# Encoder trunk on one core: a third chunk pair with seven block products in w_down, and two weight sums formed by adding DMAs

## Chip, cores and metric

The kernel runs on one core of one Trainium2 chip. The metric is the device time of one execution in microseconds (us), here the median of several runs.

## What is computed

Two residual layers, each a gated mix of three token mixers followed by an MLP with squared ReLU, and a final RMSNorm. `x` is 256 tokens by 2048 channels, float32. The change touches the last matrix product of the MLP, `w_down`:

```python
for l in range(DEPTH):                       # 2 layers
    ...
    x = x + merged @ w_out[l]
    h2 = rms_norm(x, norm2_g[l])
    u = jax.nn.relu(h2 @ w_up[l])            # 256 x 8192
    x = x + (u * u) @ w_down[l]              # w_down: 8192 x 2048
return rms_norm(x, final_g)
```

## The kernel before, in words

**Weights.** Every weight matrix is streamed once from HBM in tiles of 256 rows x 512 columns (512 KB), two chunks of 128 rows side by side in one `raw` tile (`fetch`, L165, on SP's DMA queue, four `raw` buffers). Float32 products are made from two halves of reduced width: `lead` (L171, L172) lets ScalarE round a tile to `whi` and VectorE subtract to get the rest, `wlo`. A block product is then three matmuls of 128x128 by 128x512 (`product`, L210 to L212): high by high, high by low, low by high.

**Order of the work.** `slots` is a list of tiles in the order of their use, written out by `add_unit` and `add_pair`. `run_steps` walks it: for each slot it issues the slot's matmuls and, in the middle, calls `ahead`, which converts the tile three slots further on (`AHEAD`, four `whi`/`wlo` buffers) and then fetches into every `raw` buffer that a conversion has released. Every engine executes its instructions in the order in which they are issued. Work besides the matrix products (splitting `U`, transposes, the sums named below) lies in generators, of which `side_work` runs one piece in each plain slot.

**w_up and w_down.** The 8192 features are taken in four quarters `q`. A quarter has four units of `w_up` (32 slots, `by_feature`, L228 and L229), which leave `U`, and then `w_down` for these 2048 features: two pairs of column blocks (`add_pair`), each 8 steps `s` of 256 rows. In the last quarter of a layer only one pair is done so, and the other two column blocks are plain units. That is 7 pairs in a layer, 14 in all.

**Seven products.** One step of a pair is a 2x2 by 2x2 product of blocks: two token halves, two chunks of 128 rows, two column blocks of 512. A plain step makes 8 block products in two slots (24 matmuls). For `s` in `SEVEN` it makes 7, in four slots a, b, c, d (2, 2, 2 and 1 products, 21 matmuls; `seven`). This needs four sums of token blocks (`block_sums`, L355, kept in `SU`) and four sums of weight blocks: `convert` makes them on VectorE in `T`, two at slot a (L191, L192) and two at slot b (L196, L197), from the two `raw` tiles `b0` and `b1`, which stay in use until slot b and slot d. Four of the seven products are shared sums of the results; they are kept in PSUM banks `P` over the steps and put together once per pair, by `middle_down` (L765, L770, L774), a generator that starts after the last seven-product step. `after_pair` (L797) then adds the four accumulators to `x`.

```python
SEVEN = (1, 3)
...
def ahead(i):
    convert(min(i + AHEAD, 2 * i + 1))
    fetch(st["free"] - 1 + RAW_BUFS)
```

Of the kernel before, what the change touches and what calls it, by code (L numbers as in the profile page):

```python
# [39 lines left out]
SEVEN = (1, 3)  # L40
# [31 lines left out]
def encoder_trunk(ctx: ExitStack, tc: tile.TileContext, I, out: bass.AP):  # L72
# [62 lines left out]
    slots, raws = [], []  # L135
    st = {"dma": 0, "cv": 0, "free": 0}
    raw_t, hl_t = {}, {}

    def add_raw(w, r, c):
        raws.append(w[r:r + 256, c:c + BLK])  # L140
        return len(raws) - 1
# [6 lines left out]
    def add_pair(w, r0, c0, nkc, act, sums, half, middle, after):  # L148

        u = {"act": act, "after": after, "n": nkc, "form": "pair", "sums": sums, "half": half, "middle": middle}  # L150
        for s in range(nkc // 2):
            r = [add_raw(w, r0 + 256 * s, c0 + n * BLK) for n in range(2)]
            if s in SEVEN:
                q = {"r": r}
# [6 lines left out]
    def fetch(upto):  # L161
        while st["dma"] <= min(upto, len(raws) - 1):
            j = st["dma"]
            t = raw_p.tile([128, 2, BLK], F32, tag="raw", name="raw")
            nc.sync.dma_start(out=t, in_=raws[j].rearrange("(k p) f -> p k f", p=128))  # L165
            raw_t[j] = t
            st["dma"] += 1

# [5 lines left out]
    def convert(upto):  # L174
        while st["cv"] <= min(upto, len(slots) - 1):
# [7 lines left out]
            else:  # L183
                q = sl["q"]
                if kind == "a":
                    q["b0"], q["b1"] = [raw_t.pop(r) for r in q["r"]]
                    q["T"] = one.tile([128, 4, BLK], F32, tag="merged", name="tsum")
                b0, b1, T = q["b0"], q["b1"], q["T"]
                if kind == "a":
                    nc.scalar.activation(out=hi, in_=b0, func=ACTF.Copy)  # L190
                    nc.vector.tensor_tensor(out=T[:, 1, :], in0=b1[:, 0, :], in1=b0[:, 0, :], op=ALU.subtract)  # L191
                    nc.vector.tensor_tensor(out=T[:, 0, :], in0=b1[:, 1, :], in1=T[:, 1, :], op=ALU.subtract)  # L192
                    nc.vector.tensor_tensor(out=lo, in0=b0, in1=hi.bitcast(F32), op=ALU.subtract)
                elif kind == "b":
                    nc.scalar.activation(out=hi, in_=T[:, 0:2, :], func=ACTF.Copy)
                    nc.vector.tensor_tensor(out=T[:, 2, :], in0=b1[:, 1, :], in1=b1[:, 0, :], op=ALU.subtract)  # L196
                    nc.vector.tensor_tensor(out=T[:, 3, :], in0=b0[:, 1, :], in1=T[:, 0, :], op=ALU.subtract)  # L197
                    nc.vector.tensor_tensor(out=lo, in0=T[:, 0:2, :], in1=hi.bitcast(F32), op=ALU.subtract)
                elif kind == "c":
                    lead(hi, lo, T[:, 2:4, :])  # L200
                else:
# [79 lines left out]
    def ahead(i):  # L281
        convert(min(i + AHEAD, 2 * i + 1))
        fetch(st["free"] - 1 + RAW_BUFS)

# [9 lines left out]
    def seven(u, s, kind, a, w, i):  # L294

# [53 lines left out]
    def block_sums(dst, e):  # L349
# [3 lines left out]
        for j, x0, x1, op in ((0, a21, a22, ALU.add), (1, f[:, 0, :], a11, ALU.subtract),  # L353
                              (2, a11, a21, ALU.subtract), (3, a12, f[:, 1, :], ALU.subtract)):
# [376 lines left out]
    def after_up(n):  # L731
        def f(ps):
            c = L["c"]
            if n == 0:
                c["U"] = one.tile([128, KD, 2, S], FR, tag="Y", name="U")
            U = c["U"]
# [20 lines left out]
    def middle_down(n):  # L757

        def pieces(P):
# [8 lines left out]
            def plus(tag, a, b):  # L768
# [271 lines left out]
```

## Time and profile before

| | |
|---|---|
| three runs | 2869.48 us median (2869.01 to 2870.3) |
| the profiled execution | 2870.48 us, span 2868.7 us, so 1.8 us lie around the span |
| TensorE (PE) busy | 2849.0 us, 99% of the span, granted clock 0.999 |
| VectorE (DVE), ScalarE (ACT), GpSimd (POOL) busy | 62%, 49%, 4% |
| bytes moved | 540.00 MB, 188 GB/s over the span |

Matmuls overlap: one of 512 columns is shown as 0.39 us long, and the next starts about 0.23 us after it. What a matmul costs is therefore read from the distance of starts, not from its length. The same holds in a small way for DVE and ACT, whose instructions overlap by up to a tenth of a microsecond.

### The profile page before, as it was taken

The page shows a single profiled execution, that of the slowest core. Times are in us where ns is not written, and L with a number is a line of the kernel's source. Part 1 is how long each engine was busy: PE and PEld are TensorE (multiplying, and loading weights), DVE is VectorE, ACT ScalarE, POOL GpSimd, SP SyncE. Part 2 cuts the span into 40 slices and gives each one's busy share as a digit, 9 for nine tenths or more (in the row PEclk, how much of TensorE's full clock was granted, in tenths as well). Part 3 has the DMA queues.
Part 4 walks back from the last instruction along what each step waited for, and adds up shares of the span by engine and source line. Part 5 has one row for each costly group of instructions (what it writes and reads, how often), then busy time and mean ns, then how long its engine had stood idle before and what let it go on. Part 6 is the DMA issues. An engine that isn't in the chain of part 4 may idle for free.

```text
span 2868.7 us, 35998 instructions
## 1 busy us (share of the span) xinstructions
PE 2849.0 (99%) x13858; PEld 2374.5 (83%) x13858; DVE 1778.8 (62%) x2201; ACT 1403.5 (49%) x1782; POOL 104.6 (4%) x104
## 2 busy tenths in 40 slices
PE   8999999999999999999999999999999999999998
PEld 7888888888888888888888888888888888888887
DVE  5455554555677686776644654555556876868675
ACT  5455445444554454544544554454444544444453
POOL 1000001010000000000000000011100000000001
PEclk9999999999999999999999999999999999999999
DMA  7656666665566566565676666656555565655654
GB/s 235 196 152 191 195 179 173 185 189 181 180 199 197 177 207 191 190 191 185 195 211 183 156 196 195 183 160 190 188 186 184 183 196 186 213 179 195 200 184 175
DMA packets 275804, 540.00 MB, mean 188 GB/s; under 512 B 16852, under 2 KB 17038, under 8 KB 275504
## 3 DMA queue, kind: packets, MB, share of 16 engines
q1 hardware_dynamic: 271344, 523.63, 57.7%
q0 software_dynamic: 3952, 13.28, 3.1%
q8 instruction: 108, 1.77, 0.3%
q10 hardware_dynamic: 336, 0.80, 0.1%
q14 instruction: 64, 0.52, 0.1%
HBM read 535.51 MB, written 2.13 MB: 187 GB/s over the span
## 4 chain that ended last, share of the span: by engine, by line
PE 98%; DVE 1%; ACT 0%; DMA 0%; issue 0%; POOLq 0%; DVEq 0%; POOL 0%; SPq 0%
PE acc L210 22%; PE acc L212 22%; PE acc L211 22%; PE acc L228 17%; PE acc L229 8%; PE psum L211 1%; PE psum L212 1%; PE psum L210 1%; PE ob L536 1%; PE scb L504 0%; PE xt L383 0%; PE sca L562 0%; PE oa L596 0%; PE qkt L453 0%; PE etb L526 0%
## 5 line engine op out<-in xcount | busy, mean ns | idle before, releaser
L172 DVE TENSOR_TENSOR wlo<-raw,whi 128x1024 fp32r<-128x1024 f32 (+1 forms) x964 | 1173.6, 1222 | 840.8 <-ACT whi L171 833.6
L171 ACT ACTIVATE whi<-raw 128x1024 fp32r<-128x1024 f32 (+1 forms) x964 | 1002.4, 1045 | 907.2 <-PE acc L212 556.3
L228 PE MATMUL acc<-H,whi 128*128 128x512 f32 x2048 | 724.7, 399 | 0.0
L229 PE MATMUL acc<-H,wlo 128*128 128x256 f32 x2048 | 575.2, 281 | 0.0
L210 PE MATMUL acc<-whi,H 128*128 128x512 f32 x1408 | 564.8, 401 | 0.0
L212 PE MATMUL acc<-whi,H 128*128 128x512 f32 x1408 | 550.1, 391 | 0.0
L211 PE MATMUL acc<-wlo,H 128*128 128x512 f32 x1408 | 549.5, 390 | 0.3
L228 PEld LDWEIGHTS acc<-H,whi 128*128 128x128 f32 x2048 | 384.9, 188 | 96.1 <-DVE x L705 0.6
L229 PEld LDWEIGHTS acc<-H,wlo 128*128 128x128 f32 x2048 | 387.1, 189 | 0.3
L210 PE MATMUL acc<-whi,U 128*128 128x512 f32 x856 | 334.0, 390 | 2.2 <-ACT junk L393 2.2
L211 PE MATMUL acc<-wlo,U 128*128 128x512 f32 x856 | 333.2, 389 | 0.0
L212 PE MATMUL acc<-whi,U 128*128 128x512 f32 x856 | 333.2, 389 | 0.0
L210 PEld LDWEIGHTS acc<-whi,H 128*128 128x128 f32 x1408 | 265.0, 188 | 58.6 <-issue 8.1
L212 PEld LDWEIGHTS acc<-whi,H 128*128 128x128 f32 x1408 | 264.6, 188 | 56.8
L211 PEld LDWEIGHTS acc<-wlo,H 128*128 128x128 f32 x1408 | 265.2, 188 | 52.6 <-DVE wlo L172 1.4
L210 PEld LDWEIGHTS acc<-whi,U 128*128 128x128 f32 x856 | 160.7, 188 | 36.3 <-ACT junk L393 3.0
L212 PEld LDWEIGHTS acc<-whi,U 128*128 128x128 f32 x856 | 160.7, 188 | 33.5
L211 PEld LDWEIGHTS acc<-wlo,U 128*128 128x128 f32 x856 | 160.7, 188 | 32.9
L210 PE MATMUL acc<-whi,M 128*128 128x512 f32 x256 | 101.3, 396 | 0.0
L212 PE MATMUL acc<-whi,M 128*128 128x512 f32 x256 | 99.9, 390 | 0.0
L211 PE MATMUL acc<-wlo,M 128*128 128x512 f32 x256 | 99.6, 389 | 0.0
L678 POOL TENSOR_TENSOR merged<-merged,gp 128x512 f32<-128x512 f32 x32 | 54.3, 1717 | 397.4 <-DVE gp L677 397.4
(190 smaller groups left out, 2278.1 us busy)
## 6 DMA issues: line engine op xcount, KB each, us to landing
raw<-in_w_in_dram SPq DMA_DIRECT2D x352, 512.0 KB, 4.4
raw<-in_w_up_dram SPq DMA_DIRECT2D x256, 512.0 KB, 4.2
raw<-in_w_down_dram SPq DMA_DIRECT2D x256, 512.0 KB, 4.5
raw<-in_w_out_dram SPq DMA_DIRECT2D x64, 512.0 KB, 3.8
raw<-in_w_proj_a_dram SPq DMA_DIRECT2D x24, 512.0 KB, 4.6
raw<-in_w_proj_b_dram SPq DMA_DIRECT2D x24, 512.0 KB, 4.2
raw<-in_w_proj_c_dram SPq DMA_DIRECT2D x16, 512.0 KB, 4.5
biasb<-bias_d POOLq DMA_DIRECT2D x16, 384.0 KB, 9.2
```

Of the source, the lines that this page charges most:

```text
L171: nc.scalar.activation(out=hi, in_=src, func=ACTF.Copy)
L172: nc.vector.tensor_tensor(out=lo, in0=src, in1=hi.bitcast(F32), op=ALU.subtract)
L210: nc.tensor.matmul(o, a[0], hi[:, kk, :], start=first, stop=False)
L211: nc.tensor.matmul(o, a[0], lo[:, kk, :], start=False, stop=False)
L212: nc.tensor.matmul(o, a[1], hi[:, kk, :], start=False, stop=last)
L228: nc.tensor.matmul(ps[j], hi[:, kk, fs], a[:, kc, :, :], start=first, stop=False)
L229: nc.tensor.matmul(ps[j][:, S:2 * S], lo[:, kk, fs], a[:, kc, 0, :], start=False, stop=last)
L536: nc.tensor.matmul(o[:, g, :], eT[:, 2 * g + kc, :], c["vb"][:, kc, col:col + 64], start=kc == 0, stop=kc == 1)
L678: nc.gpsimd.tensor_tensor(out=mg[:, t, cols], in0=mg[:, t, cols], in1=e, op=ALU.add)
```

## The change

`SEVEN` becomes (1, 3, 4): three of the eight steps of each pair are made with seven products. The signs of the block sums are changed so that the weight sums need only additions, and two of the four weight sums are no longer made on VectorE. `fetch_sums` loads both blocks of the first chunk into the middle of `T` (SP's queue), and a second DMA, issued by GpSimd, reads the two chunks of the second column block from HBM and adds them to what lies there. The second DMA writes where the first wrote, so it waits for it. `T` has two buffers and is loaded two seven-product steps ahead; the load into a buffer waits for slot c of the step that used it. VectorE makes the other two sums at slot a, and nothing at slot b. Of `b1` only the second chunk is still needed and loaded (256 KB in place of 512). `middle_down` is cut into six pieces in place of five.

```diff
-SEVEN = (1, 3)
+SEVEN = (1, 3, 4)
...
-            r = [add_raw(w, r0 + 256 * s, c0 + n * BLK) for n in range(2)]
+            r = [add_raw(w, r0 + 256 * s, c0 + n * BLK, half=s in SEVEN and n == 1) for n in range(2)]
             if s in SEVEN:
-                q = {"r": r}
+                q = {"r": r, "w": w[r0 + 256 * s:r0 + 256 * (s + 1), c0:c0 + 2 * BLK], "i": len(summed)}
+                summed.append(q)
...
-            nc.sync.dma_start(out=t, in_=raws[j].rearrange("(k p) f -> p k f", p=128))
+            src, half = raws[j]
+            if half:
+                nc.sync.dma_start(out=t[:, 1, :], in_=src[128:256, :])
+            else:
+                nc.sync.dma_start(out=t, in_=src.rearrange("(k p) f -> p k f", p=128))
...
+    def fetch_sums():
+
+        while L.get("T") is not None and st["sum"] < min(st["used"] + 2, len(summed)):
+            q = summed[st["sum"]]
+            if q["i"] >= L["T_end"]:
+                return
+            T = q["T"] = L["T"][:, q["i"] % 2]
+            w = q["w"]
+            nc.sync.dma_start(out=T[:, 1:3, :], in_=w[0:128, :].rearrange("p (n f) -> p n f", n=2))
+            nc.gpsimd.dma_start(out=T[:, 1:3, :], in_=w[:, BLK:2 * BLK].rearrange("(k p) f -> p k f", p=128),
+                                accum_op=ALU.add)
+            st["sum"] += 1
...
                 if kind == "a":
                     nc.scalar.activation(out=hi, in_=b0, func=ACTF.Copy)
-                    nc.vector.tensor_tensor(out=T[:, 1, :], in0=b1[:, 0, :], in1=b0[:, 0, :], op=ALU.subtract)
-                    nc.vector.tensor_tensor(out=T[:, 0, :], in0=b1[:, 1, :], in1=T[:, 1, :], op=ALU.subtract)
+                    nc.vector.tensor_tensor(out=T[:, 0, :], in0=T[:, 2, :], in1=b0[:, 0, :], op=ALU.add)
+                    nc.vector.tensor_tensor(out=T[:, 3, :], in0=T[:, 0, :], in1=b0[:, 1, :], op=ALU.add)
                     nc.vector.tensor_tensor(out=lo, in0=b0, in1=hi.bitcast(F32), op=ALU.subtract)
                 elif kind == "b":
-                    nc.scalar.activation(out=hi, in_=T[:, 0:2, :], func=ACTF.Copy)
-                    nc.vector.tensor_tensor(out=T[:, 2, :], in0=b1[:, 1, :], in1=b1[:, 0, :], op=ALU.subtract)
-                    nc.vector.tensor_tensor(out=T[:, 3, :], in0=b0[:, 1, :], in1=T[:, 0, :], op=ALU.subtract)
-                    nc.vector.tensor_tensor(out=lo, in0=T[:, 0:2, :], in1=hi.bitcast(F32), op=ALU.subtract)
+                    lead(hi, lo, T[:, 0:2, :])
                 elif kind == "c":
                     lead(hi, lo, T[:, 2:4, :])
+                    st["used"] += 1
...
         convert(min(i + AHEAD, 2 * i + 1))
         fetch(st["free"] - 1 + RAW_BUFS)
+        fetch_sums()
...
+                if "T" not in c:
+                    c["T"] = True
+                    L["T"] = one.tile([128, 2, 4, BLK], F32, tag="merged", name="tsum")
+                    L["T_end"] = len(summed) * (c["l"] + 1) // DEPTH
```

How the issue order moves is shown at two places. The first is SP's DMA queue around the first pair of a layer (`raw` with 128x2x512 is a whole tile, with 128x512 the half of `b1`; `tsum` is the load into `T`). Before, SP issues nothing but whole tiles:

```order
L165 DMA raw<-in_w_out_dram 128x2x512 x32
L165 DMA raw<-in_w_up_dram 128x2x512 x32
L165 DMA raw<-in_w_down_dram 128x2x512 x32
L165 DMA raw<-in_w_up_dram 128x2x512 x32
L165 DMA raw<-in_w_down_dram 128x2x512 x32
```

Now, from the `w_up` units on to the tiles of steps 6 and 7 of the first pair and on into the second:

```order
L182 DMA tsum<-in_w_down_dram 128x1024 x2
L170 DMA raw<-in_w_up_dram 128x2x512 x16
L170 DMA raw<-in_w_down_dram 128x2x512 x3
L168 DMA raw<-in_w_down_dram 128x512
L170 DMA raw<-in_w_down_dram 128x2x512 x2
L182 DMA tsum<-in_w_down_dram 128x1024
L170 DMA raw<-in_w_down_dram 128x2x512
L168 DMA raw<-in_w_down_dram 128x512
L170 DMA raw<-in_w_down_dram 128x2x512
L168 DMA raw<-in_w_down_dram 128x512
L182 DMA tsum<-in_w_down_dram 128x1024
L170 DMA raw<-in_w_down_dram 128x2x512 x2
```

After this last row comes another `tsum` and then seven whole tiles, the first of them those of step 6. So the first two loads into `T` lie in the middle of `w_up`, and in a pair one stands ahead of the tiles of step 3 (issued after slot c of step 1), one ahead of those of step 5 (after slot c of step 3) and one ahead of those of step 6 (after slot c of step 4).

The second place is VectorE in the same pair. Before, slots b of step 1 to b of step 3, with one `U` split of the side work between:

```order
L196 TENSOR_TENSOR tsum<-raw 128x512
L197 TENSOR_TENSOR tsum<-raw,tsum 128x512
L198 TENSOR_TENSOR wlo<-tsum,whi 128x1024
L343 TENSOR_TENSOR U<-u,U 128x2x256
L172 TENSOR_TENSOR wlo<-tsum,whi 128x1024
L172 TENSOR_TENSOR wlo<-raw,whi 128x512
L172 TENSOR_TENSOR wlo<-raw,whi 128x1024 x2
L191 TENSOR_TENSOR tsum<-raw 128x512
L192 TENSOR_TENSOR tsum<-raw,tsum 128x512
L193 TENSOR_TENSOR wlo<-raw,whi 128x1024
```

Now, slots a of step 3 to d of step 4:

```order
L208 TENSOR_TENSOR tsum<-tsum,raw 128x512
L209 TENSOR_TENSOR tsum<-tsum,raw 128x512
L210 TENSOR_TENSOR wlo<-raw,whi 128x1024
L190 TENSOR_TENSOR wlo<-tsum,whi 128x1024 x2
L190 TENSOR_TENSOR wlo<-raw,whi 128x512
L208 TENSOR_TENSOR tsum<-tsum,raw 128x512
L209 TENSOR_TENSOR tsum<-tsum,raw 128x512
L210 TENSOR_TENSOR wlo<-raw,whi 128x1024
L190 TENSOR_TENSOR wlo<-tsum,whi 128x1024 x2
L190 TENSOR_TENSOR wlo<-raw,whi 128x512
```

Each seven-product step has two sums on VectorE in place of four, both at slot a, and two such steps follow each other without a plain tile between.

## Rows read from the trace of the kernel before

**Rows 1.** The page: span, engines, and the chain that ended last by engine.

```profile
span 2868.7 us, 35998 instructions
PE 2849.0 (99%) x13858; PEld 2374.5 (83%) x13858; DVE 1778.8 (62%) x2201; ACT 1403.5 (49%) x1782; POOL 104.6 (4%) x104
...
PE 98%; DVE 1%; ACT 0%; DMA 0%; issue 0%; POOLq 0%; DVEq 0%; POOL 0%; SPq 0%
```

**Rows 2.** Windows: the first quarter's two pairs and, third, a stretch of w_up.

```profile
core 0: us, PE busy (x) PEld busy (x) DVE busy (x) ACT busy (x) POOL busy (x), PEclk, DMA share, GB/s
824.80:866.90 42.10, 42.10 (x188) 34.83 (x187) 36.28 (x44) 22.35 (x25) 0.00 (x0) 1.00 0.58 196
866.90:909.10 42.20, 42.20 (x188) 34.95 (x187) 34.39 (x39) 20.75 (x21) 0.00 (x0) 1.00 0.62 201
...
909.10:999.40 90.30, 90.30 (x512) 78.34 (x512) 57.32 (x68) 41.97 (x48) 0.00 (x0) 1.00 0.59 188
```

**Rows 3.** Timeline of PE: the first matmul of the first and second pair (start, length).

```profile
824.78 0.40 PE L210 MATMUL acc<-whi,U 128*128 128x512 f32 x1
...
867.00 0.39 PE L210 MATMUL acc<-whi,U 128*128 128x512 f32 x1
```

**Rows 4.** Groups of instructions by line and shape: conversions, weight sums, the split of SU.

```profile
L172 DVE TENSOR_TENSOR wlo<-raw,whi 128x1024 fp32r<-128x1024 f32 x936 | 1154.4, 1238 | 839.3 <-ACT whi L171 832.3
L171 ACT ACTIVATE whi<-raw 128x1024 fp32r<-128x1024 f32 x936 | 984.9, 1058 | 898.1 <-PE acc L212 547.4 <-PE acc L228 239.6 <-DMA raw<-in_w_down_dram 39.9
...
L191 DVE TENSOR_TENSOR tsum<-raw 128x512 f32<-128x512 f32 x28 | 19.3, 688 | 8.4 <-DMA raw<-in_w_down_dram 8.3
...
L343 DVE TENSOR_TENSOR SU<-ssum,SU 128x512 fp32r<-128x512 f32 x16 | 11.1, 693 | 11.2 <-ACT SU L342 11.2
```

**Rows 5.** Timeline of DVE, first pair: slots c, d of step 1; b, c of step 3.

```profile
830.67 1.22 DVE L172 TENSOR_TENSOR wlo<-tsum,whi 128x1024 fp32r<-128x1024 f32 x1
831.80 0.69 DVE L172 TENSOR_TENSOR wlo<-raw,whi 128x512 fp32r<-128x512 f32 x1
...
838.76 0.69 DVE L196 TENSOR_TENSOR tsum<-raw 128x512 f32<-128x512 f32 x1
839.37 0.69 DVE L197 TENSOR_TENSOR tsum<-raw,tsum 128x512 f32<-128x512 f32 x1
839.97 1.22 DVE L198 TENSOR_TENSOR wlo<-tsum,whi 128x1024 fp32r<-128x1024 f32 x1
841.26 1.23 DVE L172 TENSOR_TENSOR wlo<-tsum,whi 128x1024 fp32r<-128x1024 f32 x1
```

**Rows 6.** Waits: ACT for late w_down tiles (us in total, times, longest).

```profile
ACT whi L171 <- DMA raw<-in_w_down_dram: 39.9, 33, 2.8
```

**Rows 7.** DMA queues of the page: packets, MB, share of 16 engines' span.

```profile
q1 hardware_dynamic: 271344, 523.63, 57.7%
q0 software_dynamic: 3952, 13.28, 3.1%
```

**Rows 8.** Tile view of in_w_down_dram: microseconds from issue to landing.

```profile
DMA to landing us min/median/max: 3.4/4.5/7.3
```

**Rows 9.** DMA view of 2788 to 2800 us: KB each, median us to landing.

```profile
raw<-in_w_down_dram SPq DMA_DIRECT2D x5, 512.0 KB, 7.2
final_g<-in_final_g_dram POOLq DMA_DIRECT2D x1, 1024.0 KB, 7.3
```

**Rows 10.** Tile view of biasa (256 KB each, issued by POOL): issue to landing.

```profile
DMA to landing us min/median/max: 5.0/5.5/12.0
```

**Rows 11.** Tile view of biasb (384 KB each, issued by POOL): issue to landing.

```profile
DMA to landing us min/median/max: 6.6/9.2/12.3
```

**Rows 12.** Windows inside the first pair: around step 5, after the second seven-product step.

```profile
845.20:850.70 5.50, 5.50 (x26) 4.53 (x26) 4.31 (x6) 3.23 (x4) 0.00 (x0) 1.00 0.81 277
850.70:856.10 5.40, 5.40 (x25) 4.49 (x24) 5.40 (x7) 2.12 (x2) 0.00 (x0) 1.00 0.81 289
```

**Rows 13.** Groups by line: what one DMA costs POOL to issue.

```profile
L474 POOL DMA_DIRECT2D biasa<-bias_d x12 | 8.9, 741 | 2.7 <-DMA bias_d<-bt 2.7
```

More of the change, by code (lines that the diff above doesn't have):

```diff
@@ L132, in run_piece, with add_raw @@
             busy[0] -= lane[1]
-    slots, raws = [], []
-    st = {"dma": 0, "cv": 0, "free": 0}
+    slots, raws, summed = [], [], []
+    st = {"dma": 0, "cv": 0, "free": 0, "sum": 0, "used": 0}
     raw_t, hl_t = {}, {}
-    def add_raw(w, r, c):
-        raws.append(w[r:r + 256, c:c + BLK])
+    def add_raw(w, r, c, half=False):
+        raws.append((w[r:r + 256, c:c + BLK], half))
         return len(raws) - 1
@@ L186, in convert @@
                     q["b0"], q["b1"] = [raw_t.pop(r) for r in q["r"]]
-                    q["T"] = one.tile([128, 4, BLK], F32, tag="merged", name="tsum")
                 b0, b1, T = q["b0"], q["b1"], q["T"]
@@ L352, in block_sums @@
         f = w2_p.tile([128, 4, 128], F32, tag="V", name="ssum")
-        for j, x0, x1, op in ((0, a21, a22, ALU.add), (1, f[:, 0, :], a11, ALU.subtract),
-                              (2, a11, a21, ALU.subtract), (3, a12, f[:, 1, :], ALU.subtract)):
+        for j, x0, x1, op in ((0, a21, a22, ALU.subtract), (1, f[:, 0, :], a11, ALU.subtract),
+                              (2, a11, a21, ALU.subtract), (3, a12, f[:, 1, :], ALU.add)):
             nc.vector.tensor_tensor(out=f[:, j, :], in0=x0, in1=x1, op=op)
@@ L766, in add, with plus @@
                                                op0=ALU.mult, op1=ALU.add)
-            def plus(tag, a, b):
+            def plus(tag, a, b, op=ALU.add):
                 d = w2_p.tile([128, BLK], F32, tag=tag, name="usum")
-                nc.vector.tensor_tensor(out=d, in0=a, in1=b, op=ALU.add)
+                nc.vector.tensor_tensor(out=d, in0=a, in1=b, op=op)
                 return d
@@ L776, in pieces @@
             u2 = plus("V", P[6], u1)
+            yield
             add(0, 0, u1)
-            yield
-            u4 = plus("L", P[5], u2)
+            u4 = plus("L", P[5], u2, ALU.subtract)
             u3 = plus("L", P[7], u2)
             yield
-            u5 = plus("eT", P[5], u3)
+            u5 = plus("eT", P[5], u3, ALU.subtract)
+            yield
             add(0, 1, u4)
+            add(1, 0, u3)
             yield
-            add(1, 0, u3)
             add(1, 1, u5)
```

## The prediction, made before the change was run

> **What bounds the kernel now.** I read the page first, then windows, then timelines. The page [rows 1] shows TensorE (PE) busy for 99% of the span and as 98% of the chain that ended last: the time is the number of matmuls times their distance, as long as weights arrive in time. The windows [rows 2] show that this holds in the stage that is changed: in both w_down pairs of the first quarter PE is busy for all of the 42.1 and 42.2 us. What stands behind it is not idle, though: VectorE (DVE) works 36.28 of 42.1 us, against 57.32 of 90.3 in w_up, and the DMA share is 0.58 to 0.62. The matmuls that start the first and second pair lie 42.22 us apart [rows 3]; a pair has 2 x 21 + 12 x 12 = 186 matmuls, so one costs 0.227 us, a plain slot (12) 2.72 us, a seven-product step (21) 4.77 us and a plain step 5.45 us. One more view matters: ScalarE (ACT) waited 33 times, 39.9 us in all, for a w_down tile that had not landed [rows 6]. PE never felt it, since conversions run three slots ahead. But the tiles of w_down are late already, just after a seven-product step, where the DMAs move 277 to 289 GB/s [rows 12].
>
> **The change, part by part.** Times in a pair count from its first matmul; 824.78 is zero for the first.
>
> *Matmuls.* Each pair turns one plain step (24) into one of seven products (21). 14 pairs x 3 x 0.227 = **9.5 us less** on PE, all of it on the path. This is the whole gain that can be had.
>
> *VectorE.* A pair makes 3 x 2 weight sums in place of 2 x 4, two fewer, at 0.6 us between starts [rows 5]. Step 4 is converted in three and a half tiles in place of two, 1.5 x 1.13 us more (830.67 to 831.80 [rows 5]). Together +0.5 us on 36.28, in a pair of 41.5: still under 90%. Locally steps 3 and 4 need 2 x (2 x 0.6 + 3.5 x 1.13) = 10.3 us of DVE while PE spends 9.5, and DVE enters step 3 ahead; I cost it at nothing. The cover is the lead of three slots; without it 0.8 us per pair would show. DVE loses the sums at slot b, so c of a step is converted 1.2 us sooner. The 8 more splits of `SU` (0.69 us each on DVE [rows 4]) fall in w_up, where a third of DVE's time is free: nothing. The six pieces of `middle_down` fit the six plain slots left behind step 4, and the last is done before `after_pair`; ACT has half its time free. Nothing.
>
> *POOL* has no work in a pair [rows 2] and needs 0.74 us to issue a DMA [rows 13]. Waiting for the load into `T` holds nothing up there: the next norm's power comes after the last sums of a layer. Nothing.
>
> *Bytes.* A pair loses three half tiles (0.79 MB) and gets three loads and three adding reads of 0.52 MB: 8.4 MB become 10.75 MB. The price of plain traffic is 0.577 x 2868.7 / 523.63 = 3.16 us of all engines per MB on the hardware queue, 1.66 us for 512 KB; on the software queue, which an adding DMA uses, it is 0.031 x 2868.7 / 13.28 = 6.7 us per MB, 3.5 us for 512 KB [rows 7]. No row shows a DMA that adds. I bound it by these two, 1.66 and 3.5 us; as it has to read its destination besides its source, I lean to the upper half. DMA work per pair is then 17.5 x 1.66 + 3 x (1.66 to 3.5) = 34 to 40 us of 41.5. On average that fits. It does not fit evenly, and that is where I expect the loss.
>
> *The tile of step 6.* SP issues in order. After slot c of step 4 it issues a load into `T`, which waits until c is converted, and the whole tiles of step 6 stand behind it (a buffer for the first is free earlier). ACT cannot convert 4c before PE is through with 3c, whose buffers it uses: 5.45 + 4.77 + 5.45 + 3 x 1.36 = 19.75. With 1.06 us on ACT and 1.22 on DVE [rows 4, 5] 4c is done at 22.0, and SP reaches the tile at about 22.4. A w_down tile lands 3.4 us after issue at best and 4.5 in the median [rows 8]; the load ahead of it adds 1.66: 27.5 to 28.6. PE comes to step 6 at 3 x 5.45 + 3 x 4.77 = 30.65 and the conversion takes 2.3, so it must land by 28.35. That is on the edge before the adding DMA is counted. It belongs to the load that was issued after 3c: slot c of step 3 ended at 17.7 [rows 5], now about 16.5; its load lands at 20 to 21, POOL issues, and DMAs of this kind land 5.0 us (256 KB) to 9.2 us (384 KB) later [rows 10, 11], 25 to 30. So it runs beside the tile. What this does can be seen [rows 9]: beside the 1 MB of `final_g` on the software queue a w_down tile took 7.2 us where the median is 4.5, 2.7 us more. 512 KB at that price are 1.35 us, and twice as much at the upper price. The tile is late by 0 (27.5, nothing beside it) to 3 us (28.6 + 2.7). I take **1.2 us per pair**: the median landing behind the load, 28.6, and two thirds of 1.35, since part of the adding DMA is over by then.
>
> *The sums of step 4.* Their load is issued when c of step 1 is converted, at 830.67 + 1.22 - 824.78 = 7.1 before [rows 5] and about 5.9 now; it lands at 9.3 to 10.4, and the adding DMA 5.0 to 9.2 us later, at 14.3 to 19.6. Slot 4a starts at 20.44, and two sums and the conversion before it take 2.4 us, so they are needed by 18.0. The middle, 17, is in time: nothing, with 1.6 us per pair as the upper bound. All other sums are loaded 15 us or more before use.
>
> **Sum.** 2870.48 (the profiled execution, 1.0 above the median of the runs) - 9.5 + 14 x 1.2 = 2877.8; against the median some 1 us less. I say **2877 us**.
>
> **Rivals.**
> 1. *Clean gain, faster.* If the adding DMA after 3c is over when the tile of step 6 starts to move, or moves beside it without slowing it, the tile lands at 27.5 to 28.4, in time, and all 9.5 us stay: 2861. For it: average load leaves room, no PE wait in the pairs now. Against it: the tiles beside `final_g` [rows 9] and the late tiles [rows 6]. It decides at 28.35: each 0.1 us later costs 1.4 us over 14 pairs, and at 0.68 us late the gain is gone. The Trainium skill, "DMA: Bandwidth & Descriptors", section "Anatomy of one DMA — SWDGE (gpsimd) path", gives about 2.0 us plus bytes over 436 GB/s for a DMA that GpSimd issues: an estimate by it is 3.2 us for 512 KB. By that rule the DMA after 3c is over at about 24, and this rival comes true. The trace does not agree: 256 KB took 5.0 us at least [rows 10].
> 2. *Even.* The tile is late by 0.3 to 1 us: the gain is given back, 2865 to 2875.
> 3. *The sums of step 4 late too.* If an adding DMA of 512 KB is slower than the 384 KB loads [rows 11], DVE stands at the first sum of 4a, and all conversions behind it in its queue are late. At 1.6 us that is 14 x 1.6 = 22 us on top of the forecast: 2890 to 2910. For it: size, and the destination that is read. Against: 17 is the middle.
> 4. *The change doesn't do what it says*: the matmuls are counted out in the issue order (42 fewer), so only a stall elsewhere could hide them. Little.
>
> **How the numbers follow.** Within about 0.2%, 5.7 us, a measurement here cannot tell a difference from none. Forecast, 2872 to 2886: 0.36, of which 0.06 lies within that. Rival 1: 0.33. Rival 2: 0.18. Rival 3: 0.12. Rival 4: 0.01. Faster is rival 1, 0.33; the same is rival 2, rival 4 and a piece of the forecast, 0.25; slower the rest, 0.42. Cases of both signs hold most of the chance: the forecast's own range is 2872 to 2886, and the range over all reaches from 2860 (all 9.5 us, median) to 2903, which leaves out the upper part of rival 3.
>
> **What would show it.** PE's count of matmuls falls by 42, whatever the time. If I am right, PE has waits in the pairs, about 1 us long and some 14 in number, at the first matmul of step 6, put down to the conversion, and ACT waits for the w_down tile there; the DMA share around step 5 is above 0.9, and w_down tiles land later than 4.5 us in the median. Waits at 4a, with DVE's first sum waiting for the adding DMA, speak for rival 3. Pairs of 41.5 us without waits prove me wrong. So would an adding DMA that lands 3 to 4 us after its issue.

## The result and the profile after

The changed kernel took **2911.57 us** (median of 4 runs, 2907.94 to 2915.21) against 2869.24 us (4 runs, 2868.41 to 2870.3): ratio 1.0147, 95% interval 1.013 to 1.0165, slower by some 42 us. I had forecast 2877 us and a range of 2860 to 2903. The direction of the likeliest case was right, the size far off.

The page of the changed kernel: the span, what was busy, the queues, the chain's shares by engine. It answers to [rows 1] and [rows 7].

```profile
span 2913.4 us, 36216 instructions
PE 2862.0 (98%) x13816; PEld 2371.6 (81%) x13816; DVE 1794.7 (62%) x2241; ACT 1425.3 (49%) x1818; POOL 155.5 (5%) x146
q1 hardware_dynamic: 272016, 534.64, 55.8%
q0 software_dynamic: 15376, 35.30, 7.7%
PE 81%; DMA 9%; DVE 6%; issue 2%; ACT 2%; SPq 0%; POOLq 0%; ACTq 0%; DVEq 0%; POOL 0%
```

PE issued 42 matmuls fewer, as counted, but the chain runs through it for 81% where it was 98%. DMA and DVE took the difference. The software queue gained 22.02 MB and went from 3.1% [rows 7] to 7.7%. That is (0.077 x 2913.4 - 0.031 x 2868.7) / 42 = 3.2 us of all 16 engines for one adding DMA of 512 KB.

Who waited, from the view of waits (total, times, longest). The first row answers to [rows 6]; the other three have no counterpart there:

```profile
ACT whi L189 <- DMA raw<-in_w_down_dram: 132.3, 65, 8.0
PE acc L225 <- ACT whi L189: 15.0, 11, 3.0
PE acc L226 <- DVE wlo L190: 9.7, 14, 0.8
PE psum L226 <- DVE wlo L210: 5.3, 7, 2.3
```

ACT waits three times as long for w_down tiles, and now PE waits for ACT. The place is the same in 12 of the 14 pairs: the first tile of step 6. In the timelines of ACT, SP and POOL for the first pair, whose first matmul starts at 824.34, one sees how it comes about:

```profile
847.75 1.06 ACT L189 ACTIVATE whi<-raw 128x1024 fp32r<-128x1024 f32 x1 [0.23 <-PE psum L227]
855.94 1.06 ACT L189 ACTIVATE whi<-raw 128x1024 fp32r<-128x1024 f32 x1 [7.13 <-DMA raw<-in_w_down_dram]
...
847.04 0.34 SPq L182 DMA_DIRECT2D tsum<-in_w_down_dram  x1
847.43 1.93 SPq L170 DMA_DIRECT2D raw<-in_w_down_dram  x3
...
845.05 1.19 POOL L183 DMA_DIRECT2D tsum<-in_w_down_dram  x1 [9.37 <-DVE wlo L210]
```

SP issues the load into `T` at 22.7 us of the pair and the tile of step 6 right behind it at 23.1. POOL has issued the adding DMA that belongs to step 3's buffer at 20.7. ACT can start on the tile 8.5 us after its issue, at 31.6, where a landing at 28.35 would have been in time. The windows over these microseconds (columns as in [rows 2]; the last two are DMA share and GB/s) show what the DMA engines did:

```profile
846.50:848.00 1.50, 1.50 (x9) 1.23 (x8) 1.50 (x3) 1.26 (x2) 0.00 (x0) 1.00 0.69 81
848.00:850.00 2.00, 2.00 (x10) 1.67 (x9) 1.93 (x2) 0.81 (x1) 0.00 (x0) 1.00 1.04 188
850.00:852.00 2.00, 2.00 (x10) 1.67 (x9) 0.07 (x1) 0.00 (x0) 0.00 (x0) 1.00 1.05 368
```

From 848 to 850 all engines are busy and move 188 GB/s; two microseconds later it is 368. The slow stretch is the adding DMA's: by the trace's packet records no packet of SP's queue began between 847.19 and 850.28, although its load had been issued at 847.04 (in e2_no_add, below, the first packet of this load came 1.0 us after its issue).

Where the waits are longer, a second loss follows that I had not counted at all. The same place in the fourth pair, in the timeline of PE:

```profile
1082.51 0.39 PE L227 MATMUL acc<-whi,U 128*128 128x512 f32 x1
1085.88 0.80 PE L225 MATMUL acc<-whi,U 128*128 128x512 f32 x1 [2.98 <-ACT whi L189]
1087.14 0.80 PE L226 MATMUL acc<-wlo,U 128*128 128x512 f32 x1 [0.47 <-DVE wlo L190]
1087.73 0.63 PE L227 MATMUL acc<-whi,U 128*128 128x512 f32 x1
1088.16 0.63 PE L225 MATMUL acc<-whi,U 128*128 128x512 f32 x1
...
1092.24 0.39 PE L226 MATMUL acc<-wlo,U 128*128 128x512 f32 x1
1092.46 0.39 PE L227 MATMUL acc<-whi,U 128*128 128x512 f32 x1
```

and in the windows of the same stretch:

```profile
1085.50:1092.00 6.50, 5.66 (x13) 4.09 (x13) 5.92 (x7) 3.89 (x5) 0.00 (x0) 0.50 0.97 253
1092.00:1100.00 8.00, 8.00 (x37) 6.61 (x36) 7.41 (x10) 3.19 (x3) 0.00 (x0) 1.00 0.78 238
```

After the wait the matmuls stand 0.43 us apart in place of 0.227, until 1092: the granted clock is 0.50 there, 1.2 in place of 2.4 GHz, and 1.00 right after.

From the starts of all 128x512 matmuls of the 14 pairs I added up what each distance has over 0.227 us, by the slot before which it lies; distances of 0.30 to 0.47 us make a column of their own, which is half speed and a few short waits. The columns are microseconds over all 14 pairs; the kernels below the second are the experiments.

| kernel | step 1 | steps 3, 4 | steps 5, 6 | half speed | ends of pairs | sum | median, us |
|---|---|---|---|---|---|---|---|
| before | 0 | 0.3 | 0 | 0.1 | 2.5 | 2.9 | 2869.2 |
| after | 1.4 | 7.1 | 31.3 | 14.7 | 4.2 | 58.6 | 2911.6 |
| e1_late_sums | 30.1 | 3.0 | 0 | 12.8 | 4.3 | 50.2 | 2908.9 |
| e2_no_add | 0.6 | 2.6 | 4.7 | 2.7 | 4.2 | 14.8 | 2873.6 |
| e3_dve_sums | 0 | 13.0 | 0 | 3.0 | 4.2 | 20.3 | 2880.9 |
| e4_two_steps | 0 | 0 | 0 | 0 | 2.5 | 2.5 | 2869.4 |
| e5_swap | 8.9 | 6.1 | 0.6 | 4.4 | 4.7 | 24.7 | 2887.0 |
| e6_plain_sw | 0 | 0.8 | 27.3 | 11.9 | 4.0 | 44.0 | 2895.1 |
| e7_one_by_dma | 0 | 7.5 | 0 | 3.1 | 4.3 | 14.8 | 2873.9 |
| e8_three_bufs | 0 | 3.1 | 0 | 0.6 | 4.2 | 7.8 | 2867.4 |
| e9_places_a | 0 | 0 | 0 | 0 | 3.9 | 3.9 | 2861.5 |
| e9_places_b | 17.0 | 0 | 0 | 5.8 | 3.9 | 26.7 | 2880.9 |
| e10_two_by_dma | 0.6 | 0 | 0 | 0.1 | 4.0 | 4.8 | 2861.8 |
| e11_half_add | 0.6 | 2.8 | 24.0 | 9.2 | 4.0 | 40.6 | 2894.9 |

The columns come from the profiled execution of each kernel, the median from all its runs. The profiled executions of the changed kernel, e6_plain_sw and e11_half_add lay 3.6, 9.2 and 3.7 us above their medians.

The two traces differ by 2913.4 - 2868.7 = 44.7 us. The table accounts for 58.6 - 2.9 - 9.5 (the matmuls saved) = 46.2 of them; 30.0 of the 31.3 us at steps 5 and 6 lie at the first tile of step 6.

### The profile page after: what moved, and what is told of

It is laid out like the page before. It is cut to its first block, busy times and chain, and to the rows that moved or that the text cites. A ratio compares the mean times of both kernels' runs of the same rounds, so it can differ in the third digit from the quotient of the medians.

```text
span 2913.4 us, 36216 instructions
## 1 busy us (share of the span) xinstructions
PE 2862.0 (98%) x13816; PEld 2371.6 (81%) x13816; DVE 1794.7 (62%) x2241; ACT 1425.3 (49%) x1818; POOL 155.5 (5%) x146
## 4 chain that ended last, share of the span: by engine, by line
PE 81%; DMA 9%; DVE 6%; issue 2%; ACT 2%; SPq 0%; POOLq 0%; ACTq 0%; DVEq 0%; POOL 0%
PE acc L225 17%; PE acc L226 17%; PE acc L227 17%; PE acc L243 16%; PE acc L244 8%; DMA raw<-in_w_down_dram 5%; DMA tsum<-in_w_down_dram 4%; DVE wlo L190 3%; ACT whi L189 1%; PE ob L553 1%; DVE wlo L210 1%; PE scb L521 0%; DVE tsum L208 0%; DVE x L819 0%; PE xt L400 0%
## 5 line engine op out<-in xcount | busy, mean ns | idle before, releaser
L190 DVE TENSOR_TENSOR wlo<-raw,whi 128x1024 fp32r<-128x1024 f32 (+1 forms) x950 | 1146.2, 1214 | 847.3 <-ACT whi L189 842.7
L189 ACT ACTIVATE whi<-raw 128x1024 fp32r<-128x1024 f32 (+1 forms) x950 | 980.1, 1038 | 928.1 <-PE acc L227 498.2
L225 PE MATMUL acc<-whi,U 128*128 128x512 f32 x772 | 307.0, 398 | 18.9 <-ACT whi L189 15.0
L226 PE MATMUL acc<-wlo,U 128*128 128x512 f32 x772 | 307.2, 398 | 9.6 <-DVE wlo L190 9.3
L227 PE MATMUL acc<-whi,U 128*128 128x512 f32 x772 | 304.6, 395 | 0.0
L225 PEld LDWEIGHTS acc<-whi,U 128*128 128x128 f32 x772 | 147.2, 191 | 55.5 <-ACT whi L189 20.0
L226 PEld LDWEIGHTS acc<-wlo,U 128*128 128x128 f32 x772 | 147.4, 191 | 45.4 <-DVE wlo L190 15.4
L227 PEld LDWEIGHTS acc<-whi,U 128*128 128x128 f32 x772 | 147.7, 191 | 30.9
L183 POOL DMA_DIRECT2D tsum<-in_w_down_dram x42 | 50.7, 1220 | 1238.5 <-DMA tsum<-in_w_down_dram 1110.1
L189 ACT ACTIVATE whi<-tsum 128x1024 fp32r<-128x1024 f32 x84 | 87.1, 1053 | 33.3 <-DVE tsum L208 19.2
L225 PE MATMUL acc<-whi,M 128*128 128x512 f32 x256 | 101.2, 395 | 0.0
L190 DVE TENSOR_TENSOR wlo<-tsum,whi 128x1024 fp32r<-128x1024 f32 x84 | 99.6, 1219 | 2.1 <-ACT whi L189 2.1
```

Source lines behind the costliest of these rows:

```text
L183: nc.gpsimd.dma_start(out=T[:, 1:3, :], in_=w[:, BLK:2 * BLK].rearrange("(k p) f -> p k f", p=128), accum_op=ALU.add)
L189: nc.scalar.activation(out=hi, in_=src, func=ACTF.Copy)
L190: nc.vector.tensor_tensor(out=lo, in0=src, in1=hi.bitcast(F32), op=ALU.subtract)
L225: nc.tensor.matmul(o, a[0], hi[:, kk, :], start=first, stop=False)
L226: nc.tensor.matmul(o, a[0], lo[:, kk, :], start=False, stop=False)
L227: nc.tensor.matmul(o, a[1], hi[:, kk, :], start=False, stop=last)
```

## The theories

**A**: the DMAs that GpSimd issues take the 16 DMA engines almost for themselves for some 3 us, and the plain tiles behind them are late by that much; long waits also cost TensorE its clock. **B**: two seven-product steps in a row are more than VectorE can do in their time. **C**: the tile of step 6 is late only because SP issues it behind a load that waits for slot c of step 4.

## The experiments

### e1_late_sums: the loads for the next pair put behind the tiles of steps 6 and 7

```diff
+SUMS_AT = ((0, 1), (5, 0), (6, 1))
-        fetch_sums()
+        sl = slots[i]
+        if sl["u"]["form"] != "pair":
+            fetch_sums()
+        elif (sl["s"], sl.get("n")) in SUMS_AT:
+            fetch_sums(1)
```

> Theory A (the adding DMAs hold the DMA engines some 3 us each, the plain tiles behind them stand, and waits of several us also lower TensorE's granted clock). Here the loads and adding DMAs for the next pair are issued later, after the conversions for the tiles of steps 6 and 7, so that the first tile of step 6 stands behind nothing on SP: A expects the waits of TensorE at step 6 to go (30 us over the pairs of the changed kernel), the half-speed stretches behind them too, and some short waits at slot a of step 4 to remain: 2858 to 2866 us, faster than the kernel before. Theory B (two steps of seven products in a row are too much for VectorE): nothing that loads VectorE is changed, so 2890 us or more. Theory C (the tile of step 6 is late only because it stands behind a load that waits on SP): the same as A here; the next kernel tells those two apart.

Measured: 2908.88 us, ratio 1.0139 (1.0124 to 1.0154). The time is one that B allowed, but not for B's reason: VectorE does not lag, it waits for a DMA itself. The waits at step 6 are gone, as A and C said, and the same 30 us stand at slot a of step 1 in the second pairs. The rows of SP, POOL and DVE around the second pair's start, from the timelines:

```profile
852.12 0.47 SPq L183 DMA_DIRECT2D tsum<-in_w_down_dram  x1
...
858.99 1.19 POOL L184 DMA_DIRECT2D tsum<-in_w_down_dram  x1 [25.30 <-DVE wlo L192]
...
869.83 0.69 DVE L210 TENSOR_TENSOR tsum<-tsum,raw 128x512 f32<-128x512 f32 x1 [7.82 <-DMA tsum<-in_w_down_dram]
```

The load goes out at 852.12, the adding DMA can be issued at 858.99, and VectorE has its operand at 869.83: 17.7 us from SP's issue to use. I had looked at where the DMAs were in the way and not at how early their sums are wanted. What follows: load and adding DMA are a chain, of 12.5 us by the median landings in the changed kernel (4.5 and 8.0) and of 17.7 here, and a place too late costs as much as one too early.

### e2_no_add: without the adding DMAs

```diff
-            nc.gpsimd.dma_start(out=T[:, 1:3, :], in_=w[:, BLK:2 * BLK].rearrange("(k p) f -> p k f", p=128),
-                                accum_op=ALU.add)
```

> The changed kernel without the adding DMAs; it leaves out the addition of the second column block to the two sums, so its output is another. Everything else, with the order on SP and the load into T ahead of the tiles of step 6, is as in the changed kernel. Theory A (the adding DMA holds the engines): waits at step 6 at most 0.3 us per pair, 2860 to 2868 us. Theory C (order on SP alone): still 1 us per pair or more at step 6, 2880 us or more. Theory B (VectorE): 2890 us or more, since VectorE works as much.

Measured: 2873.56 us, ratio 1.0013 (1.0003 to 1.0022): between A's range and C's. In the first pair the tile of step 6 stands behind the load into `T` just as before, and lands in time (timelines of SP and ACT; the first line merges seven tiles, of which this is the first):

```profile
847.39 11.94 SPq L170 DMA_DIRECT2D raw<-in_w_down_dram  x7
...
852.88 1.06 ACT L187 ACTIVATE whi<-raw 128x1024 fp32r<-128x1024 f32 x1 [3.81 <-DMA raw<-in_w_down_dram]
```

Both tiles were issued at 847.4, and ACT starts on them at 852.88 and 855.94: the adding DMA costs this tile 3.0 us. That this is near its own 3.2 us of engine time does not show that the tile waited for all of it. The trace marks the landing of a DMA in 16 parts, and the tile counts as landed with the last. Without the adding DMA the parts of this tile landed from 851.81 to 852.77; with it, 15 of them from 853.23 to 853.60 and the last at 855.84. So some 1 us of the 3 is lost by all parts and 2 us by one straggler alone. VectorE has the same work as in the changed kernel and 38 of the 42 us are gone, so B is not the cause there. The 4.7 us that stay at steps 5 and 6, all of them in second pairs, are what the place behind the load costs alone.

### e3_dve_sums: three steps with all sums on VectorE

```diff
-SEVEN = (1, 3)
+SEVEN = (1, 3, 4)
```

(of the kernel before)

> The kernel before with three steps of seven products and no adding DMA: all four sums on VectorE, 2 more sums than before per pair (4 x 0.6 us per step). Theory A and C: TensorE has 42 matmuls (9.5 us) less and no DMA wait beyond those of before: 2860 to 2875 us. Theory B: VectorE with 8 more sums of 0.6 us per pair than a plain step would have cannot keep up over steps 3 and 4: 2890 us or more, with VectorE's conversions as the releaser of TensorE's waits.

Measured: 2880.91 us, ratio 1.0041 (1.0026 to 1.0056), between the two. No DMA wait reaches PE; what does, in every one of the 14 pairs, is slot b of step 4, in the view of waits:

```profile
PE psum L211 <- DVE wlo L198: 9.3, 14, 0.7
PEld psum L211 <- DVE wlo L198: 15.3, 14, 1.1
```

0.83 us per pair, 11.6 in all. (This kernel makes 12 sums per pair on VectorE in place of 8, four more and not two.) B is true of this form of the kernel: the adding DMAs took off VectorE a load that would have shown. It is a smaller one than what they brought.

### e4_two_steps: adding DMAs, two steps

```diff
-SEVEN = (1, 3, 4)
+SEVEN = (1, 3)
```

(of the changed kernel)

> The adding DMAs alone, with two steps of seven products as before (SEVEN = (1, 3)): the matmuls are those of the kernel before. Theory A: after slot c of step 3 the adding DMA for the next pair still holds the engines for some 3 us beside the tiles of steps 5 and 6, but the slots there are plain ones from step 4 on and the load into T waits for nothing behind them: short waits, 2869 to 2885 us, never faster than 2867. Theory C: no load waits for 4c ahead of the tiles of step 6, so no wait: 2869 us. Theory B: VectorE has two sums less per step: 2869 us.

Measured: 2869.41 us, ratio 1.0 (0.999 to 1.0009). So 28 adding DMAs, half of which run beside the tiles of steps 5 and 6, cost nothing. ACT feels them, PE does not:

```profile
ACT whi L189 <- DMA raw<-in_w_down_dram: 92.0, 70, 4.7
```

A's short waits were not there. An adding DMA is not dear as such: here the tiles of steps 5 and 6 stand behind no load that waits for a slot of step 4, and what they come later the lead of three slots covers.

### e5_swap: only the load after 4c behind the tiles of step 6

```diff
+SUMS_AT = ((0, 1), (2, 1), (4, "a"))
```

(with the gate of e1, by the kind of slot where there is no tile number)

> Only SP's order is altered: the load into T that follows slot c of step 4 is issued one slot later, behind both tiles of step 6. The adding DMAs stay, and so does the load after slot c of step 3. The earlier kernel without adding DMAs kept 8 us of waits in the pairs beyond those of the kernel before, so order alone is not all. Theory A (the adding DMA after 3c holds the engines while the tiles of steps 5 and 6 are due, and the load only adds to it): the waits at step 6 shrink from 30 us by the load's own 1.4 us in each of 12 pairs and a little more, to 8 to 16 us; 2878 to 2898 us. Theory C (the place behind that load is the cause): waits at step 6 under 2 us in all, 2858 to 2868 us.

Measured: 2887.04 us, ratio 1.0058 (1.0043 to 1.0073), inside A's range of time, but the waits at the first tile of step 6 are none at all, which was C's number. The tile of the first pair is issued at 845.27, ahead of the load, and lands 5.1 us later, although by the packet records the adding DMA runs from 848 to past 852 in this kernel too, side by side with SP's packets. ACT starts on it at 850.48, 5.5 us sooner than in the changed kernel:

```profile
850.48 1.06 ACT L191 ACTIVATE whi<-raw 128x1024 fp32r<-128x1024 f32 x1 [1.23 <-DMA raw<-in_w_down_dram]
```

The time that was lost instead lies at steps 1, 3 and 4 (15.0 us), where sums and tiles were now late. Neither theory alone holds: at step 6 it takes the place behind the load **and** a GpSimd DMA at that moment. With both 30.0 us, with the place alone (e2) 2.6, with the adding DMA alone (e5) none.

### e6_plain_sw: the same DMA without adding

```diff
-            nc.gpsimd.dma_start(..., accum_op=ALU.add)
+            nc.gpsimd.dma_start(...)
```

> The changed kernel with each adding DMA turned into a plain DMA of the same 512 KB, queue and place (it leaves out the addition: T holds the second operand alone). If it is the adding that makes the packets slow (178 ns per 2 KB where plain ones take 84), the engines are held 1.4 us in place of 2.9 and waits at step 6 fall to 5 to 12 us: 2872 to 2890 us. If it is the way over GpSimd's queue, the cost stays: 2900 us or more, with the packets of that queue as long as before. If the traffic were free, it would be the kernel without these DMAs: 2873 us.

Measured: 2895.08 us, ratio 1.0092 (1.0074 to 1.0111), between what the two cases said. Not adding halves the engine time: (0.054 x 2902.5 - 0.031 x 2868.7) / 42 = 1.6 us per DMA, and the DMA lands 6.3 us after its issue in the median where the adding one takes 8.0. The rows for it, of the page and of the view of DMAs (size, median us to landing), SP's issue of the tile of the first pair (again the first of seven), and ACT's wait for it:

```profile
q0 software_dynamic: 10000, 35.30, 5.4%
...
tsum<-in_w_down_dram POOLq DMA_DIRECT2D x42, 512.0 KB, 6.3
...
848.22 13.61 SPq L170 DMA_DIRECT2D raw<-in_w_down_dram  x7
...
855.97 1.06 ACT L188 ACTIVATE whi<-raw 128x1024 fp32r<-128x1024 f32 x1 [6.06 <-DMA raw<-in_w_down_dram]
```

Yet the tile is late again: ACT starts on it 7.8 us after its issue, against 8.5 with adding and 5.5 without the DMA, and 27.3 us stay at step 6. So a GpSimd DMA in front of the tile delays it, adding or not. The adding still costs: by the medians of all runs the plain DMAs make the kernel 21.5 us slower than e2_no_add, the adding ones 38.0. No run puts the same 512 KB at this moment on another queue, so it is not shown that it has to be GpSimd's.

### e11_half_add: half the bytes

```diff
-            nc.gpsimd.dma_start(out=T[:, 1:3, :], in_=w[:, BLK:2 * BLK].rearrange("(k p) f -> p k f", p=128),
-                                accum_op=ALU.add)
+            nc.gpsimd.dma_start(out=T[:, 2, :], in_=w[128:256, BLK:2 * BLK], accum_op=ALU.add)
```

> The changed kernel with half of each adding DMA, 256 KB in place of 512 (it leaves out the addition to the sum for slot b; T holds a bare operand there). Order, places and loads as in the changed kernel. New form of theory A (what delays the tile of step 6 is the stretch of some 3 us in which a GpSimd DMA of 512 KB takes the engines, on top of the load ahead): the stretch is about 1.6 us, the tile lands some 1.4 us sooner, and of the 2.5 us that TensorE lost per pair at step 6 about 1.1 are left: 10 to 16 us of waits there, few of them long, so half-speed stretches of 5 us or less: 2880 to 2892 us. If a GpSimd DMA costs by its start and not by its bytes: 25 us or more at step 6 and 2895 us or more. If the waits at step 6 go altogether: 2873 us, as without adding DMAs.

Measured: 2894.91 us, ratio 1.0096 (1.0082 to 1.011): a miss for the bytes, and just short of the case in which the start of a DMA costs. 22.9 us stay at the first tile of step 6. It is not uniform: in the first pair ACT starts on the tile 6.1 us after its issue, where the kernel without adding DMAs has 5.5, while second pairs lost up to 3.6 us. The tile of the first pair, in the timelines of SP and ACT:

```profile
847.23 12.63 SPq L170 DMA_DIRECT2D raw<-in_w_down_dram  x7
...
853.28 1.06 ACT L188 ACTIVATE whi<-raw 128x1024 fp32r<-128x1024 f32 x1 [4.38 <-DMA raw<-in_w_down_dram]
```

In five of the twelve pairs the loss is 0.05 to 1.0 us, in seven 1.6 to 3.6. Engine time per DMA is 1.6 us, as for the plain one. Over the four kernels 0, 1.6 (half and plain) and 3.2 us of engine time gave 2.6, 23 to 27 and 30 us at step 6: the loss grows with the engine time, but not in proportion, and half of it costs most of the loss. By the medians of all runs half an adding DMA costs 21.4 us over e2_no_add and a whole one 38.0.

The landing parts say more. Medians over the first tiles of step 6 in the 12 pairs, in us from SP's issue to the landing of a part:

| kernel | engine time per GpSimd DMA | first part | eighth | last: the tile is there |
|---|---|---|---|---|
| e2_no_add | 0 | 4.3 | 4.8 | 5.4 |
| e11_half_add | 1.6 | 5.0 | 6.0 | 7.2 |
| e6_plain_sw | 1.6 | 4.5 | 5.3 | 7.8 |
| after | 3.2 | 5.9 | 6.4 | 7.8 |

The whole adding DMA makes all parts of the tile late, by 1.6 us. The plain one leaves the first half nearly in time and makes the last part late, by 2.4 us; half an adding DMA lies between. So the tile pays for its slowest part, which the length of the GpSimd DMA doesn't tell. Why the parts come so unevenly, and why second pairs suffer more, these runs don't show; it stays open.

### e7_one_by_dma: only step 4's sums by DMA

```diff
+BY_DMA = (4,)
...
-                if kind == "a":
+                if kind == "a" and not q["dma"]:
+                    nc.vector.tensor_tensor(out=T[:, 1, :], in0=b0[:, 0, :], in1=b1[:, 0, :], op=ALU.add)
+                    nc.vector.tensor_tensor(out=T[:, 0, :], in0=T[:, 1, :], in1=b1[:, 1, :], op=ALU.add)
...
+        if sl["u"]["form"] != "pair" or (sl["s"], sl.get("n")) == (6, 1):
+            fetch_sums()
```

> Three steps of seven products, but only step 4 gets its two sums by DMA, steps 1 and 3 form all four on VectorE as in the kernel before; the one load and adding DMA of a pair stand behind the last slot of step 6, 15 us or more before the next pair needs buffers and some 40 us before use. Theory A: no place is left at which an adding DMA holds back a tile that is needed: no waits beyond those of before, and VectorE's sums at step 4, which cost 0.85 us per pair where all were on VectorE, are two fewer: 2858 to 2864 us. Theory B (VectorE over steps 3 and 4): 0.5 us per pair or more stay, 2867 us or more.

Measured: 2873.88 us, ratio 1.0012 (1.0003 to 1.0022): B's case. No wait is left at steps 5 to 7, and 7.5 us at steps 3 and 4 most of it released by VectorE's conversion for slot 4a, up to 0.8 us per pair. Two sums off VectorE at step 4 alone are not enough.

### e8_three_bufs, e9_places_a, e9_places_b: a buffer for each step, and three choices of place

The three loads of a pair get rows of their own in `T`, and the other two sums share two rows, so a sum can be loaded a whole pair ahead. The three kernels differ in one line:

```diff
-                    L["T"] = one.tile([128, 2, 4, BLK], F32, tag="merged", name="tsum")
+                    L["T"] = one.tile([128, 8, BLK], F32, tag="merged", name="tsum")
...
-            T = q["T"] = L["T"][:, q["i"] % 2]
+            T, k = L["T"], 1 + 2 * (q["i"] % 3)
...
+SUMS_AT = ((0, 1), (5, 0), (7, 0))
+SUMS_AT = ((2, 1), (6, 0), (7, 1))
+SUMS_AT = ((4, "d"), (6, 0), (7, 1))
```

(one line of the last three each, in the order of the names above)

> All three steps by adding DMAs, but each with a buffer of its own, so that a sum is loaded a whole pair ahead, and with its loads at three places chosen for room: behind slot c of step 1, behind the first tile of step 6, and behind the first tile of step 7's place. Theory A (it is the time at which the adding DMAs run that costs, not their bytes: 42 x 2.9 us of engines fit into the pairs on average): the waits at step 6, at 1a and at 4a all go, 2858 to 2864 us. If the pairs lack DMA time as a whole (DMA share near 1 with adding DMAs counted): waits move to other tiles and 2875 us or more remain.

> All three steps by adding DMAs with a buffer each, as in the kernel with three buffers, but with the loads behind slot c of step 3, and behind tiles of steps 7 and 7's successor, in place of behind slot c of step 1 and so on. Theory A in its new form (each DMA that GpSimd issues takes the engines for some 3 us, and it costs only where a tile in front of TensorE has less than that to spare): the waits left at 4a of the second pairs (3.1 us in all) came from the load and the adding DMA behind step 1, which run beside the tiles of steps 3 and 4, so they go: 2861 to 2866 us. Against it: the DMA behind 3c now runs beside the tiles of steps 5 and 6, as in the changed kernel, and if a pair lacks DMA time as a whole, short waits turn up there: 2867 to 2875 us.

> The same with the first load of a pair behind slot d of step 4's successors, so that all three loads and adding DMAs of a pair fall between the tiles of step 6 and the next pair's step 1. New form of theory A: no waits at steps 4 to 6; but three times 3 us of adding DMA and three loads stand close together, so that tiles of step 7 or of the next pair's steps 0 and 1 may be late: between 2862 us (they have the lead) and 2880 us (1a or 1b late by 1 us in the second pairs).

Measured: 2867.38 us, ratio 0.999 (0.9981 to 1.0), between its two cases, with 3.1 us left at 4a, for the first; **2861.54 us, ratio 0.9976 (0.9966 to 0.9985)** for the second; 2880.94 us, ratio 1.0042 (1.0029 to 1.0054), for the third, which lost 17.0 us at step 1, just beyond the upper end of its expectation (six second pairs, 1.5 to 3.3 us each at 1a). The second is what the change was worth: all 42 adding DMAs are there, with the same bytes and the same engine time as in the changed kernel, and the windows of the first quarter's pairs, 41.5 and 41.3 us long, show PE busy throughout (against 42.1 and 42.2 in [rows 2]):

```profile
824.50:866.00 41.50, 41.50 (x185) 34.36 (x184) 35.55 (x41) 24.33 (x26) 2.39 (x2) 1.00 0.67 216
866.00:907.30 41.30, 41.30 (x185) 34.23 (x185) 35.82 (x41) 22.45 (x23) 3.53 (x3) 1.00 0.92 265
...
q0 software_dynamic: 15376, 35.30, 7.6%
```

The DMA share is 0.92 in the second pair, and still nothing waits. So neither the bytes nor the count of adding DMAs made the changed kernel slow, but the moments at which they were issued. Between the second and the third of these kernels only one place differs, and 19.4 us.

### e10_two_by_dma: steps 3 and 4 by DMA, step 1 on VectorE

```diff
+BY_DMA = (3, 4)
+SUMS_AT = ((5, 0), (7, 0))
...
-                q = {"r": r, "w": w[r0 + 256 * s:r0 + 256 * (s + 1), c0:c0 + 2 * BLK], "i": len(summed)}
+                q = {"r": r, "dma": s in BY_DMA, "k": 5}
```

> Steps 3 and 4 by adding DMAs, loaded a pair ahead behind the tiles of steps 6 and 7; step 1 forms its sums on VectorE. Both theories together: VectorE has the two sums less just where two steps of seven products stand in a row (0.85 us per pair with all on VectorE, 0.4 us with one step by DMA), and one adding DMA per pair less takes the engines: no waits beyond those of before except at the end of the last pairs, 2860 to 2864 us. If VectorE at step 3 after a step 1 of its own still lags, 4a shows 0.3 us per pair: 2866 us.

Measured: **2861.82 us, ratio 0.9974 (0.9964 to 0.9985)**, as expected. It gets by with 28 adding DMAs; the DMA share in the second pair is lower than in e9_places_a, and it is as fast within what the runs tell apart. Both beat the kernel before and the changed one:

```profile
866.00:907.30 41.30, 41.30 (x184) 34.21 (x183) 36.41 (x41) 22.47 (x23) 2.39 (x2) 1.00 0.81 241
```

## Why the prediction was wrong, point by point

*Matmuls.* Right: 42 fewer, 9.5 us. e9_places_a and e10_two_by_dma show it whole: a pair without waits has 41.5 us.

*The tile of step 6.* Right in place, cause and decisive hour, and **wrong in size: this is the step that failed**. I had SP at the tile at 22.4 (23.1), the load landing and POOL issuing at 20 to 21 (20.7), the tile landing at 28.6 behind the load alone (28.2 in the first pair of e2_no_add), and 28.35 as the last moment in time. Then I let the adding DMA cost it two thirds of 1.35 us, 0.9, because the tiles beside `final_g` [rows 9] had shared the engines with a DMA of twice the size. It cost 3.0 there, and 2.4 in the median of the 12 pairs (7.8 us from issue to landing against 5.4). The tile of the first pair landed at 31.5, 3.1 us too late: the upper end of my own bounds, and I took the middle. In sum 30.0 us in 12 pairs, 2.5 each, where I had 14 x 1.2 = 16.8; the single pairs, behind whose step 4 no load follows, lost nothing there. The row beside `final_g` was the wrong measure: it is a median over five tiles, and the one tile that matters here is as late as the last of its 16 parts.

The Trainium skill, "DMA: Bandwidth & Descriptors", section "Issuing engines are not separate DMA queues", says that DMAs from any issuing engine run on the same 16 engines and interleave. The first half agrees with the windows, where the DMA share is 1.04 at 188 GB/s while the adding DMA runs. The second agrees with the packet records of e5_swap, in which packets of both queues begin within the same half microsecond from 848 to 850; in the changed kernel no packet of SP's queue began from 847.19 to 850.28.

*The clock.* Missing from the sum: 14.7 us in the half-speed column. I had priced a wait as the wait. In the fourth pair 4.5 us of waiting at step 6 were followed by ten distances of 0.43 us in place of 0.227, 2.0 us more; the mean granted clock of the whole run is 0.994 against 0.999. Not every such wait was followed by half speed: seven pairs have a stretch at 0.50, but the first and the eleventh, with 3.1 and 3.3 us of waiting, have none. In the kernels whose waits inside a pair stayed under 2 us (e2, e3, e5, e7) the granted clock fell nowhere in the pairs; their 2.7 to 4.4 us in that column are short waits.

*The sums of step 4.* Taken as nothing, with 1.6 us per pair as bound. Steps 3 and 4 lost 7.1 us in all, 0.5 per pair. The adding DMAs landed 8.0 us after issue in the median, inside the 5.0 to 9.2 I had; part of the wait was for tiles, not for sums: by the view of waits VectorE's first sum stood 10.8 us in all for an adding DMA and 14.6 us for a tile.

*VectorE.* Right for the changed kernel, and only there: with the DMAs' two sums off it, no pair of e9_places_a waits for VectorE. Without them it is 0.83 us per pair, the number I had given for a lost cover (0.8).

*`middle_down`.* Called nothing. In all twelve kernels with step 4 in seven products PE waits 1.4 to 2.2 us longer at the ends of pairs, all but a trace of it behind the very last pair. In the changed kernel VectorE is busy there with `middle_down` (L786) and a conversion until 2859.4, while the pair's last matmul started at 2857.84; no run tests whether the sixth piece is the cause.

*Price of the adding DMA.* 1.66 to 3.5 us of engines, upper half: measured 3.2. Average load fits, as said (share 0.92 at most).

*Rivals.* The clean gain did not come. The Trainium skill, "DMA: Bandwidth & Descriptors", section "Anatomy of one DMA — SWDGE (gpsimd) path", gives for it an estimate of 3.2 us from issue to landing for 512 KB; the trace does not agree, with 8.0 in the median, and 6.3 for a plain one in e6_plain_sw. Rival 3 (2890 to 2910) came nearest to the time, for another reason.

The sum that would have been right: 2870.5 - 9.5 + 30.0 at step 6 + 14.6 of clock + 8.2 at steps 1, 3 and 4 + 1.3 at steps 5 and 6 beside that + 1.7 at the ends = 2916.8, against 2915.2 for the profiled execution (its span and the 1.8 us around it).

## What to carry to other kernels

When a change puts DMAs on GpSimd's queue beside tiles that are due, do not price the first tile behind such a DMA with a share of its bytes: here it landed 1.8 to 2.4 us later in the median and 3.5 to 4.0 us later in the worst pair, for 256 KB as for 512. The tile counts as landed with the last of its 16 parts, and these came up to 4.4 us apart (e6_plain_sw and e11_half_add). Ask for each DMA which tile that is. The moment of issue is a cost of its own: the same 42 DMAs made this kernel 42 us slower or 7 us faster, by the slots behind which they are issued and the buffer rows that leave the choice; one such slot alone was worth 19 us. And a wait of several microseconds on TensorE can cost more than itself, so a sum of waits wants a term for the clock.

## What had not been expected of the hardware

- A plain GpSimd DMA of 512 KB delayed the tile behind it by 2.4 us in the median, as much as an adding one, though it used 1.6 us of the engines and the adding one 3.2. Half an adding DMA still left 22.9 of 30.0 us.
- One part of 16 can hold a tile back: in the first pair of the changed kernel 15 parts had landed by 853.60 us and the last landed at 855.84.
- From SP's load to a usable sum it was 17.7 us in e1_late_sums: 6.9 until POOL could issue, 10.8 until VectorE ran, for twice 512 KB.
- POOL needs 1.2 us to issue an adding DMA (50.7 us for 42), against 0.74 us for a plain one [rows 13].
- Granted clock 0.50 in the window from 1085.5 to 1092 us, behind a wait of 3 us, and 1.00 again from one matmul to the next (0.43 us apart until 1092.00, 0.23 from there on).
